# A hybrid attention and RG-LRU block on one core: the first stages written out in order for all five engines, with fewer, larger weight loads and two gates moved in between the compression products

## The chip, the cores and the metric

The kernel runs on one core of a Trainium2 chip. The metric is the device time of one execution in microseconds (us), as the median of several runs. Engines are named as in the profile: PE (TensorE), ACT (ScalarE), DVE (VectorE), POOL (GpSimd), SP (the engine that here only issues transfers).

## What is computed

One layer of a decoder: sequence 512, width 1024, float32. The input is normed; one wide projection gives queries, six key and value projections, gates and the recurrent branch. The stretch that the change touches is the norm, those projections, and `compress_blocks` (32 tokens of 64 channels, in steps of 16, through a small two-layer net), called once for keys and once for values:

```
def rms_norm(x, w):
    var = jnp.mean(xf * xf, axis=-1, keepdims=True)
    return (xf * lax.rsqrt(var + EPS) * w.astype(jnp.float32)).astype(x.dtype)
...
    xn = rms_norm(x, norm1_w[l])
    z = xn @ w_in[l]
    (q, k_c, v_c, k_s, v_s, k_w, v_w, g_nsa, xr, gr, g_a, g_b) = jnp.split(z, IN_SPLITS, axis=-1)
...
    blocks = jnp.concatenate([kb[:, :-1], kb[:, 1:]], axis=2) + pos[:, None, :]
    flat = blocks.transpose(0, 1, 3, 2, 4).reshape(B, nc, N_KV_GROUPS, CMP_BLOCK * HEAD_DIM)
    c = jax.nn.gelu(flat @ w1) @ w2
...
    merged = jax.nn.sigmoid(g_a) * (attn @ w_up_attn[l]) + jax.nn.sigmoid(g_b) * (rnn @ w_up_rnn[l])
    x = x + merged @ w_out[l]
    hn = rms_norm(x, norm2_w[l])
    x = x + jnp.square(jax.nn.relu(hn @ mlp_w1[l])) @ mlp_w2[l]
```

Behind the projections come attention over compressed, selected and windowed keys (8 heads, 4 blocks of 128 queries), the recurrence, the merge, and a squared-ReLU MLP.

## The kernel before, in words

**Precision.** Each float32 product is three matmuls: every operand is split into a rounded part (hi) and the rest (lo), and PE adds hi·hi, lo·hi and hi·lo. A unit such as `k0`, `kc` or a gate `g` is 8 blocks of 128 rows times 3 matmuls of 128x512: 24 matmuls (`unit_mm`, L422 to L424: weight hi, weight lo, activation lo).

**Weights.** A weight tile is 128x1024 (512 KB). From job 4 on it comes twice: POOL issues a load into `whi` (L191), ACT writes minus its rounded part into `wlo` (L218), and POOL issues a second load that adds the source to it (L219). Only the four query tiles come raw (`wraw`, SP's queue, L201) and are split by ACT (L361) and DVE (L363).

**Order of the first stages.** PE and SP follow the written order. ACT, DVE and POOL are ordered by a scheduler. The written order on PE is: warm-up (L115); 96 query matmuls (L381), with the sum of squares (`n_ss`, L325) and the broadcast of the norm's factor (`n_b`, L343) near their end; `k0`, `k1`; 96 matmuls of `v` (L520 to L522); and then what the string `MID = "kvSTcccccccc"` says: `kc`, `vc` (k, v), start of the attention lanes (S scores, T transposes and products), eight compression units (c, 8 matmuls `hid` each, L630). After it come 16 gates `g`. Lanes go one step ahead at each `tick()`; in `unit_mm` a tick comes after every `step[0]` blocks, and `GSTEP = (2,) * 16` gives 6 fill matmuls per tick in all gates.

**The norm.** ACT squares `xT` (L369), POOL adds the squares up (`sqa`, L366 and L370), PE sums over partitions (L325), POOL takes the power (L337). `q`, `k0`, `k1`, `v`, `kc`, `vc` are multiplied out from the un-normed input `xwh`/`xwl`, and the factor `rb` (L389) is applied when they leave the accumulator; the gates use the normed input `xnh`/`xnl` (L401 to L403; POOL makes `xnl`). DVE gathers `kc` and `vc` into the block layout `T` while multiplying by `rb` (L570, 16 instructions of 64x248), and ACT and DVE split `T` into `tc` (L574, L575). The finish of a compression unit (`hs` L580, `hq`, `hx`, `kp`) is a chain over ACT, DVE and PE.

Of the kernel before, what the change touches and what calls it, by code (L numbers as in the profile page):

```python
# [7 lines left out]
F32 = mybir.dt.float32  # L8
# [7 lines left out]
P = 128  # L16
# [29 lines left out]
KLP = "dp"  # L46
QLP = "dd"
# [4 lines left out]
MID = "kvSTcccccccc"  # L52
# [10 lines left out]
CLO = "ppdd" * 4  # L63
GSTEP = (2,) * 16
# [11 lines left out]
def kernel(ctx: ExitStack, tc: tile.TileContext, a, out: bass.AP):  # L76
# [9 lines left out]
    ctx.enter_context(tc.manual_schedule(engines={nc.tensor.engine, nc.sync.engine}))  # L86

# [38 lines left out]
    def job(src, n=1024, lo="dd", hi="aa"):  # L126
        jobs.append((src, n, lo + hi))
# [3 lines left out]
    job(a["wz"][0])  # L131
    job(a["wz"][1])
    VK = ((0, 3), (3, 6), (6, 8))
    for k0, k1 in VK:
        job(a["wv"][:, k0 * 280:k1 * 280], (k1 - k0) * 280)
    job(a["wz"][2])
    job(a["wz"][3])
    mid = {"g": [a["wz"][t] for t in range(20, 36)], "c": [a["cw1"][c] for c in range(8)]}
    for x in MID:
        if x in mid:  # L140
            job(mid[x].pop(0), lo=CLO[2 * (7 - len(mid["c"])):][:2] if x == "c" else "dd")
    for w in mid["g"]:
        job(w)
    tail = [a["wz"][4 + 2 * c + kind] for kind, c in RORDER] + [a["wua"][n] for n in range(4)]
    for n, w in enumerate(tail):
        if XA <= n < XB:
            job(w, lo=XLO, hi=XHI)
        else:
            job(w)
# [26 lines left out]

    def dma_to(i):
        while nxt["dma"] <= min(i, len(jobs) - 1):
            n = nxt["dma"]
            src, w, _ = jobs[n]  # L180
            if isinstance(src, tuple):
# [7 lines left out]
            if n >= 4:  # L189
                hi = wt("whi")  # L190
                pool.dma_start(hi[:, :w], src)  # L191
                raws[n] = hi
                nxt["dma"] += 1
                continue
            r = wt("wraw", F32)
            raws[n] = r
            if n < 4:
                for h in range(2):
                    k = 2 * n + h
                    sp.dma_start(xT[k], a["xT"][k])  # L200
                    sp.dma_start(r[:, h * S:(h + 1) * S], a["wq"][k])  # L201
# [9 lines left out]
    def conv_to(i, parts=1):  # L211
        while nxt["conv"] <= min(i, len(jobs) - 1):
# [3 lines left out]
            if not isinstance(src, tuple):  # L216
                hi, lo = raws[n], wt("wlo")
                act.activation(lo[:, :w], f(hi[:, :w]), AF.Copy, scale=-1.0)  # L218
                pool.dma_start(lo[:, :w], src, accum_op=OP.add)  # L219
                convs[n] = (hi, lo)  # L220
# [99 lines left out]
    def ss_mm(sqs, nt, name):  # L320
        ps = pt("av", name + "_ss", [P, nt])
        n = len(sqs)
        for m, sq in enumerate(sqs):
            for i in range(nt):
                pe.matmul(ps[:, i:i + 1], lhsT=sq[:, i * P:(i + 1) * P], rhs=ones[:, 0:1],  # L325
                          start=(m == 0 and i == 0), stop=(m == n - 1), skip_group_check=True)
        return ps

    def ss_pow(ps, nt, power, name, r=None):
# [4 lines left out]
        if power == -1:  # L334
            dve.reciprocal(r, ms)
        else:
            pool.tensor_tensor(r, ms, mhalf[:, :nt], op=OP.pow)  # L337
# [8 lines left out]

    sqa = tt("sqa")
    qps = [pt("mm", "q0"), pt("mm", "q1"), pt("s", "q2"), pt("s", "q3")]
    rb = const.tile([P, S], F32, name="rb")
    xwh, xwl, wq = [], [], []  # L350
    for k in range(KD):
        if k % 2 == 0:
            raw = raws[k // 2]
            wh2 = wt("whi")
            wl2 = wt("wlo")
            nxt["use"] += 1
            nxt["conv"] += 1
# [16 lines left out]
    rc = const.tile([P, NT], F32, name="rc")
    rch = const.tile([P, NT], F32, name="rch")
    for k in range(KD):
        for t in range(3):
            for j in range(4):
                cs = slice(j * P, (j + 1) * P)
                l_, r_ = ((wq[k][0], xwh[k]), (wq[k][1], xwh[k]), (wq[k][0], xwl[k]))[t]  # L380
                pe.matmul(qps[j], lhsT=l_[:, cs], rhs=r_, start=(k == 0 and t == 0),  # L381
                          stop=(k == KD - 1 and t == 2))
        if k == 5:
            ss = ss_mm([sqa], NT, "n1")
            rs_ = ss_pow(ss, NT, -0.5, "n1", rc)
            dve.tensor_scalar(rch, rc, 0.5, None, op0=OP.mult)
        if k == 6:
            rb_ps = ss_bcast(rs_, NT, "n1")
            act.copy(rb, rb_ps)  # L389
    dma_to(4 + 3)  # L390
    conv_to(5)

    xnh, xnl = [], []
    for k in range(KD):
        xnh.append(rt("X", f"xnh{k}", F32R))
        xnl.append(rt("X", f"xnl{k}", F32R))

    def xn_lane():
        for k in range(KD):
            x32 = tt("x32")  # L400
            dve.scalar_tensor_tensor(x32, xT[k], v("n1", k), rb, op0=OP.mult, op1=OP.mult)  # L401
            act.copy(xnh[k], x32)
            pool.tensor_tensor(xnl[k], x32, f(xnh[k]), op=OP.subtract)  # L403
            yield

    qs = [rt("A", f"qs{h}", F32R) for h in range(NH)]

    def q_evac(j):
        q32 = tt("q32")
        dve.tensor_tensor(q32, qps[j], rb, op=OP.mult)  # L410
        e, o = qs[2 * j], qs[2 * j + 1]
        act.copy(e[0:64], q32[0:64])
        act.copy(o[64:128], q32[64:128])
        (pool if QLP[0] == "p" else dve).tensor_tensor(e[64:128], q32[0:64], f(e[0:64]), op=OP.subtract)
# [797 lines left out]
```

## Time and profile before

| what | value |
|---|---|
| median of 3 runs | 838.39 us (837.63 to 839.85) |
| profiled execution | 839.27 us |
| its span, first to last instruction | 837.6 us |
| PE busy | 788.0 us, 94% |
| DVE busy | 596.9 us, 71% |
| ACT, POOL busy | 439.2 us, 358.6 us |

The profiled execution is 1.7 us longer than its span: the time around the instructions. Read the profile by stages: the page's 40 slices show in which of them PE is not full, the table of stretches gives each stage's own busy times and granted clock, the waits of PE say what it waited for, and the timeline when each thing began.

### The profile page before, as it was taken

The numbers are of one execution on the slowest core, as the hardware profiler recorded it, in microseconds if no ns is written. First come the engines' busy times: TensorE is split into PE (matmuls) and PEld (weight loads), VectorE is DVE, ScalarE is ACT, GpSimd is POOL, SyncE is SP. The second block draws the span as 40 slices with busy tenths as digits, with TensorE's granted clock in tenths as the row PEclk, the third lists the DMA queues.
The fourth block names the chain that finished last, engine by engine and source line by source line (L and its number), as shares of the span: only waits on it lengthen the run. The fifth ranks groups of instructions, "written<-read, shape, count | busy, mean of one in ns | idle before, by whom it ended". The sixth has DMA issues, their size and how long they took to land. (4 is left out here: it accounts for less than half of the span.)

```text
span 837.6 us, 10414 instructions
## 1 busy us (share of the span) xinstructions
PE 788.0 (94%) x3626; PEld 640.5 (76%) x3626; DVE 596.9 (71%) x989; ACT 439.2 (52%) x793; POOL 358.6 (43%) x379
## 2 busy tenths in 40 slices
PE   6996599999999999999996999999999999999986
PEld 3895478877777888788884888788878888888764
DVE  8488435767776576776479847877777777777895
ACT  7255445655555689796343464444444444435343
POOL 5566322111111222222458228574747373736842
PEclk9998689999999999999997999999999999999988
DMA  6758996555444678778990574657575747486302
GB/s 212 186 138 190 249 234 146 106 115 106 102 101 105 154 159 191 173 163 173 206 300 11 182 171 76 165 131 178 126 188 118 194 108 204 97 232 146 102 0 100
DMA packets 43828, 126.43 MB, mean 151 GB/s; under 512 B 5120, under 2 KB 5376, under 8 KB 43776
## 3 DMA queue, kind: packets, MB, share of 16 engines
q0 software_dynamic: 26208, 94.58, 51.4%
q1 hardware_dynamic: 17568, 31.19, 11.3%
q8 instruction: 28, 0.46, 0.2%
q14 instruction: 24, 0.20, 0.1%
HBM read 123.66 MB, written 2.10 MB: 150 GB/s over the span
## 5 line engine op out<-in xcount | busy, mean ns | idle before, releaser
L218 ACT ACTIVATE wlo<-whi 128x1024 fp32r<-128x1024 f32 (+2 forms) x91 | 95.6, 1051 | 61.9 <-PE ur L423 12.2
L209 DVE TENSOR_TENSOR wlo<-braw,whi 128x512 fp32r<-128x512 f32 x120 | 97.1, 840 | 40.2 <-issue 35.2
L278 POOL TENSOR_TENSOR braw<-braw,braw 128x512 f32<-128x512 f32 x64 | 98.5, 1552 | 25.6 <-DVE wlo L209 22.7
L423 PE MATMUL h<-hnh,wlo 128*128 128x512 f32 x256 | 100.5, 392 | 2.1 <-DMA wlo<-in_w_dram 1.8
L422 PE MATMUL h<-hnh,whi 128*128 128x512 f32 x256 | 99.8, 390 | 0.0
L424 PE MATMUL h<-hnl,whi 128*128 128x512 f32 x256 | 99.7, 390 | 0.0
L206 ACT CAST whi<-braw 128x512 fp32r<-128x512 f32 x120 | 69.2, 615 | 57.2 <-POOL braw L278 41.2
L191 POOL DMA_DIRECT2D whi<-in_wz_dram x36 | 22.2, 616 | 162.2 <-PE g L424 118.0
L1079 DVE SCALAR_TENSOR_TENSOR x<-p,r,x 128x512 f32<-128x512 f32 x112 | 80.1, 741 | 3.1 <-PE p L1045 3.0
L423 PEld LDWEIGHTS h<-hnh,wlo 128*128 128x128 f32 x256 | 48.0, 188 | 14.7 <-DMA wlo<-in_w_dram 4.9
L424 PEld LDWEIGHTS h<-hnl,whi 128*128 128x128 f32 x256 | 48.1, 188 | 10.1 <-DVE hnl L1017 0.2
L422 PEld LDWEIGHTS h<-hnh,whi 128*128 128x128 f32 x256 | 48.1, 188 | 9.9
L422 PE MATMUL g<-xnh,whi 128*128 128x512 f32 x128 | 55.6, 434 | 0.0
L1045 PE MATMUL p<-whi,sl 128*128 128x512 f32 x128 | 50.7, 396 | 3.1 <-DVE sl L209 3.1
L1042 PE MATMUL p<-whi,sh 128*128 128x512 f32 x128 | 50.6, 396 | 2.0 <-ACT sh L206 2.0
L423 PE MATMUL g<-xnh,wlo 128*128 128x512 f32 x128 | 50.6, 395 | 1.3 <-DMA wlo<-in_wz_dram 1.3
L424 PE MATMUL g<-xnl,whi 128*128 128x512 f32 x128 | 50.9, 398 | 0.0
L1044 PE MATMUL p<-wlo,sh 128*128 128x512 f32 x128 | 50.4, 394 | 0.0
L721 DVE TENSOR_REDUCE mx<-sb 128x1 f32<-128x384 f32 (+3 forms) x44 | 28.2, 641 | 28.0 <-PE sb L718 27.8
L219 POOL DMA_DIRECT2D wlo<-in_w_dram x32 | 28.0, 876 | 43.6 <-ACT wlo L218 39.7
L1066 DVE TENSOR_TENSOR h<-h 128x512 f32<-128x512 f32 x32 | 38.3, 1198 | 11.2 <-ACT h L1065 11.2
L219 POOL DMA_DIRECT2D wlo<-in_wz_dram x36 | 31.9, 887 | 32.0 <-ACT wlo L218 29.0
(323 smaller groups left out, 2126.0 us busy)
## 6 DMA issues: line engine op xcount, KB each, us to landing
whi<-in_wz_dram POOLq DMA_DIRECT2D x36, 512.0 KB, 3.8
wlo<-in_wz_dram POOLq DMA_DIRECT2D x36, 512.0 KB, 7.0
braw<-in_w_dram SPq DMA_DIRECT2D x64, 256.0 KB, 5.2
whi<-in_w_dram POOLq DMA_DIRECT2D x32, 512.0 KB, 4.6
wlo<-in_w_dram POOLq DMA_DIRECT2D x32, 512.0 KB, 6.4
whi<-in_cw_dram POOLq DMA_DIRECT2D x8, 512.0 KB, 4.8
wlo<-in_cw_dram POOLq DMA_DIRECT2D x8, 512.0 KB, 8.1
whi<-in_wur_dram POOLq DMA_DIRECT2D x8, 512.0 KB, 3.6
```

Source lines behind the costliest of these rows:

```text
L206: act.copy(hi, src)
L209: (pool if eng == "p" else dve).tensor_tensor(lo, src, f(hi), op=OP.subtract)
L218: act.activation(lo[:, :w], f(hi[:, :w]), AF.Copy, scale=-1.0)
L219: pool.dma_start(lo[:, :w], src, accum_op=OP.add)
L278: pool.tensor_tensor(o, i0, i1, op=OP.subtract)
L422: pe.matmul(ps, lhsT=wh[:, c], rhs=ah[k][:, sl], start=(first and i == 0), stop=False)
L423: pe.matmul(ps, lhsT=wl[:, c], rhs=ah[k][:, sl], start=False, stop=False)
L424: pe.matmul(ps, lhsT=wh[:, c], rhs=al[k][:, sl], start=False, stop=(last and i == n - 1))
L1042: pe.matmul(ps, lhsT=ah[:, qs_], rhs=wh[:, ws], start=(fresh and m == 0), stop=False, skip_group_check=True)
L1044: pe.matmul(ps, lhsT=ah[:, qs_], rhs=wl[:, ws], start=False, stop=False, skip_group_check=True)
L1045: pe.matmul(ps, lhsT=al[:, qs_], rhs=wh[:, ws], start=False, stop=(end and m == 1), skip_group_check=True)
L1079: dve.scalar_tensor_tensor(x2[i][c], ps, 0.5 if n == "w" else r2[:, i:i + 1], x2[i][c], op0=OP.mult, op1=OP.add)
```

## The change

All five engines follow a written order from the start to the letter T in `MID`; after it ACT, DVE and POOL are ordered by the scheduler as before. Within that stretch:

- **Query preparation** goes block by block (k): ACT casts the weight, then the input; DVE takes both rests. The squares are taken by ACT from a second, row-wise copy of the input (`xq`, 8 loads of 256 KB on SP's queue), each with its row sum (`accum_out`); POOL's additions and the 8 `n_ss` matmuls go.
- **Weights.** Jobs 4 to 8 (`k0`, `k1`, `v`) and the eight compression tiles (`cw1`) come once, raw, on SP's queue, and are split by ACT (cast) and DVE (subtract). `v`'s and the compression's raw tiles share two buffers ("big"). `kc`, `vc` and the gates keep the two loads on POOL's queue.
- **POOL's arithmetic** on `sqa`, `xnl` and `kl` goes; DVE makes `xnl` and `kl`, ACT copies the mirrored half of `kl`.
- **`kc` and `vc`** are multiplied from the normed input, so the gather into `T` needs no factor; ACT does it, as 16 copies.
- **`MID`** puts gate `g0` ahead of the compression units and `g1` between its halves, and starts the lanes there. The last three gates tick after every block: 3 fill matmuls per tick.

```diff
-MID = "kvSTcccccccc"
+MID = "kvgccccSTgcccc"
+EAHEAD = (0, 0)
...
-GSTEP = (2,) * 16
+GSTEP = (2,) * 13 + (1,) * 3
...
+    early = tc.manual_schedule(engines={pe.engine, sp.engine, act.engine, dve.engine, pool.engine})
+    early.__enter__()
...
+    job(a["wz"][0], by="hw")
+    job(a["wz"][1], by="hw")
+        job(a["wv"][:, k0 * 280:k1 * 280], (k1 - k0) * 280, by="hw")
...
+    def load(n):
+        src, w, _ = jobs[n]
+        if n in hw:
+            raws[n] = const.tile([P, 1024], F32, name="vraw", tag="big", bufs=2) if n > 5 else wt("wraw", F32)
+            sp.dma_start(raws[n][:, :w], src)
+        else:
+            raws[n] = wt("whi")
+            pool.dma_start(raws[n][:, :w], src)
...
+    def conv(n):
+        src, w, _ = jobs[n]
+        if n in hw:
+            hi, lo = wt("whi"), wt("wlo")
+            q = w // 2
+            for m in range(2):
+                sl = slice(m * q, (m + 1) * q)
+                act.copy(hi[:, sl], raws[n][:, sl])
+                pump(1, lambda sl=sl: dve.tensor_tensor(
+                    lo[:, sl], raws[n][:, sl], f(hi[:, sl]), op=OP.subtract))
+            pump(0)
+        else:
+            hi, lo = raws[n], wt("wlo")
+            act.activation(lo[:, :w], f(hi[:, :w]), AF.Copy, scale=-1.0)
+            pool.dma_start(lo[:, :w], src, accum_op=OP.add)
+        convs[n] = (hi, lo)
...
+    xq = {}
+    for i in range(NT):
+        for c in range(2):
+            xq[i, c] = tt(f"xq{i}{c}")
+            sp.dma_start(xq[i, c], a["xt"][i, c])
+    posr = const.tile([P, 2, 16], F32, name="posr")
+    sp.dma_start(posr, a["pos"])
+    craw = []
+
+    def c_load():
+        t = const.tile([P, 1024], F32, name=f"craw{len(craw)}", tag="big", bufs=2)
+        sp.dma_start(t, a["cw1"][len(craw)])
+        craw.append(t)
...
+    def ss_pow(ps, nt, name, r):
         ms = st(name + "_ms", [P, nt])
-        dve.tensor_scalar(ms, ps, 1.0 / D, EPS, op0=OP.mult, op1=OP.add)
-        if r is None:
-            r = st(name + "_r", [P, nt])
...
-        if k == 0:
-            pool.tensor_tensor(sqa, xT[k], xT[k], op=OP.mult)
-        else:
-            sq = tt("sq")
-            act.activation(sq, xT[k], AF.Square)
-            pool.tensor_tensor(sqa, sqa, sq, op=OP.add)
...
-            pool.tensor_tensor(xnl[k], x32, f(xnh[k]), op=OP.subtract)
...
+        next(consts, None)
+    for i in range(NT):
+        for c in range(2):
+            act.activation(xq[i, c], xq[i, c], AF.Square, accum_out=ssq1[:, i, c:c + 1])
...
+            conv(4)
+            rs_ = ss_pow(ssq1, NT, "n1", rc)
+            dve.tensor_scalar(rch, rc, 0.5, None, op0=OP.mult)
+        if k == 5:
+            conv(5)
+        if k == 6:
+            rb_ps = ss_bcast(rs_, NT, "n1")
+            act.copy(rb, rb_ps)
+            conv(6)
+            conv(7)
+            load(9)
+            load(8)
+            c_load()
+        if k == 1:
+            load(4)
+            load(5)
+            load(6)
+            load(7)
...
+    def xn_part(k0, k1):
+        for k in range(k0, k1):
+            x32 = tt("x32")
+            dve.scalar_tensor_tensor(x32, xT[k], v("n1", k), rb, op0=OP.mult, op1=OP.mult)
+            act.copy(xnh[k], x32)
+            pump(1, lambda k=k, x32=x32: dve.tensor_tensor(xnl[k], x32, f(xnh[k]), op=OP.subtract))
...
+    conv(9)
+    load(10)
+    xn_part(0, 4)
     xw_unit("k0", lambda ps: k_evac(ps, 0), "t")
+    xn_part(4, 6)
+    conv(8)
+    c_load()
+    load(11)
+    conv(10)
+    xn_part(6, 8)
     xw_unit("k1", lambda ps: k_evac(ps, 1), "t")
-    lanes.append(xn_lane())
+    pump(0)
+    conv(11)
...
-                for m in range(2):
-                    o_ = T[w][hf * 64:hf * 64 + 64, m * 8:m * 8 + 8, g, 0:NCB - 1].rearrange("p j n -> p n j")
-                    dve.tensor_tensor(o_, pv[:, m:m + NCB - 1, hf::2], rv[:, m:m + NCB - 1, hf::2], op=OP.mult)
-        for c in range(4):
-            t = ring.tile([P, 4, 2, DH], F32R, name=f"tc{c}", tag="T", bufs=8)
-            src = T[w][:, c * 4:c * 4 + 4].rearrange("p j g n -> p j (g n)")
-            act.copy(t[:, :, 0], src)
-            dve.tensor_tensor(t[:, :, 1], src, f(t[:, :, 0]), op=OP.subtract)
...
+        for m in range(2):
+            if m and not w:
+                conv(12)
+            T = tt("T", [P, 8, NG, NCB])
+            for g in range(NG):
+                dve.tensor_copy(T[:, :, g, NCB - 1], posr[:, w, m * 8:m * 8 + 8])
+            for g in range(NG):
+                pv = ps[g * 64:g * 64 + 64].rearrange("p (n s) -> p n s", s=16)
+                for hf in range(2):
+                    o_ = T[hf * 64:hf * 64 + 64, :, g, 0:NCB - 1].rearrange("p j n -> p n j")
+                    act.copy(o_, pv[:, m:m + NCB - 1, hf::2])
+            for c in (2 * m, 2 * m + 1):
+                t = ring.tile([P, 4, 2, DH], F32R, name=f"tc{c}", tag="T", bufs=8)
+                src = T[:, (c % 2) * 4:(c % 2) * 4 + 4].rearrange("p j g n -> p j (g n)")
+                act.copy(t[:, :, 0], src)
+                pump(1, lambda t=t, src=src: dve.tensor_tensor(t[:, :, 1], src, f(t[:, :, 0]), op=OP.subtract))
+                tc_[w, c] = t
...
+    def c_split():
+        n = c_split.n
+        if n == 8:
+            return
+        c_split.n += 1
+        hi, lo = wt("chi"), wt("clo")
+        for m in range(2):
+            sl = slice(m * S, (m + 1) * S)
+            act.copy(hi[:, sl], craw[n][:, sl])
+            pump(1, lambda sl=sl: dve.tensor_tensor(lo[:, sl], craw[n][:, sl], f(hi[:, sl]), op=OP.subtract))
+        cconv.append((hi, lo))
+        if len(craw) < 8:
+            c_load()
+    c_split.n = 0
...
+    extra = {"k": lambda: (load(12), c_split()), "v": c_split, "g": c_split}
     for x in MID + "g" * (16 - MID.count("g")):
+        if ng < 1 and x in extra:
+            extra[x]()
         if x == "c":
+            if not cconv:
+                c_split()
+            pump(0)
             next(cmp)
+            c_split()
+            if len(craw) > 5 and 13 not in raws:
+                load(13)
+            if len(craw) > 6 and 13 not in done:
+                conv(13)
             tick()
         elif x == "T":
+            pump(0)
+            early.__exit__(None, None, None)
+            ahead[:] = DMA_AHEAD, CONV_AHEAD
             lanes.append(tr_lane())
         elif x == "S":
             lanes.append(s_lane())
         elif x == "k":
-            xw_unit("kc", lambda ps: t_evac(ps, 0), "av")
+            z_unit("kc", lambda ps: t_evac(ps, 0), "av")
         elif x == "v":
-            xw_unit("vc", lambda ps: t_evac(ps, 1), "av")
+            z_unit("vc", lambda ps: t_evac(ps, 1), "av")
```

**ACT in the query preparation.** In these rows `whi` is the cast of a query weight block, `xwh` that of an input block, `sq` a square. Before:

```order
L362 ACTIVATE xwh_135<-xT_93,vec 128x512
L362 ACTIVATE xwh_142<-xT_94,vec 128x512
L362 ACTIVATE xwh_153<-xT_95,vec 128x512
L369 ACTIVATE sq<-xT_94 128x512
L369 ACTIVATE sq<-xT_95 128x512
L362 ACTIVATE xwh_162<-xT_96,vec 128x512
L369 ACTIVATE sq<-xT_96 128x512
L362 ACTIVATE xwh_173<-xT_97,vec 128x512
L369 ACTIVATE sq<-xT_97 128x512
L361 CAST whi<-wraw 128x512 x6
```

Now:

```order
L437 CAST whi<-wraw 128x512
L438 ACTIVATE xwh_170<-xT_96,vec 128x512
L401 ACTIVATE ez<-ez 128x8
L437 CAST whi<-wraw 128x512
L438 ACTIVATE xwh_185<-xT_99,vec 128x512
L437 CAST whi<-wraw 128x512
```

The first weight cast stood behind five input casts and four squares; now it is the first of the stage, and no square stands ahead of a cast.

**ACT at the end of the compression's first half.** `hs` is the copy that begins the finish of the key half, `pr` an exponential of the score lane, `chi` the cast of a raw compression tile. Before:

```order
L218 ACTIVATE wlo<-whi 128x1024
L727 ACTIVATE pr,sm<-sb,nb 128x128 x8
L218 ACTIVATE wlo<-whi 128x1024
L580 COPY hs<-hid_811 128x256
L218 ACTIVATE wlo<-whi 128x1024
L206 CAST th<-tp 128x512
```

Now:

```order
L854 CAST chi<-craw_792 128x512 x2
L854 CAST chi<-craw_851 128x512 x2
L193 ACTIVATE wlo<-whi 128x1024
L854 CAST chi<-craw_895 128x512 x2
L854 CAST chi<-craw_913 128x512 x2
L626 COPY hs<-hid_881 128x256
L773 ACTIVATE pr,sm<-sb,nb 128x128 x8
```

`hs` and the first exponentials now stand behind the casts of the sixth and seventh raw tile (895 and 913).

**PE in one slot of the last three gates.** `g` are the fill matmuls, `av` a product of the attention lane, `sb` a score product, `tp` transposes. Before:

```order
L422 MATMUL g_2456<-xnh_342,whi 128x512
L423 MATMUL g_2456<-xnh_342,wlo 128x512
L424 MATMUL g_2456<-xnl_343,whi 128x512
L422 MATMUL g_2456<-xnh_344,whi 128x512
L423 MATMUL g_2456<-xnh_344,wlo 128x512
L424 MATMUL g_2456<-xnl_345,whi 128x512
L762 MATMUL av<-th,vs_489 128x512
L762 MATMUL av<-tl,vs_489 128x512
L714 MATMUL sb<-kh_427,qs_361 128x512
L716 MATMUL sb<-kl_428,qs_361 128x512
L718 LDWEIGHTS identb
L718 MATMUL sb<-tri,identb 128x128
```

Now:

```order
L508 MATMUL g_2430<-xnh_415,whi 128x512
L509 MATMUL g_2430<-xnh_415,wlo 128x512
L510 MATMUL g_2430<-xnl_416,whi 128x512
L808 MATMUL av<-th,vs_584 128x512
L808 MATMUL av<-tl,vs_584 128x512
L760 MATMUL sb<-kh_503,qs_428 128x512
L762 MATMUL sb<-kl_504,qs_428 128x512
L764 LDWEIGHTS identb
L764 MATMUL sb<-tri,identb 128x128
L793 MATMUL tp<-ident,pr 128x128 x4
```

Three of the six fill matmuls in a slot are gone; the lane's own matmuls are the same.

## Rows read from the trace of the kernel before

**Rows 1.** The page: busy time by engine, and the granted clock in 40 slices.

```profile
PE 788.0 (94%) x3626; PEld 640.5 (76%) x3626; DVE 596.9 (71%) x989; ACT 439.2 (52%) x793; POOL 358.6 (43%) x379
...
PEclk9998689999999999999997999999999999999988
```

**Rows 2.** Stretches in us; length, busy PE, PEld, DVE, ACT, POOL; clock, DMA share, GB/s.

```profile
0.00:12.32 12.32, 4.45 (x10) 1.34 (x10) 9.18 (x29) 8.01 (x16) 5.12 (x10) 1.00 0.84 288
12.32:38.59 26.27, 26.10 (x111) 21.17 (x112) 15.11 (x16) 10.31 (x17) 16.34 (x20) 1.00 0.65 176
38.59:49.70 11.11, 11.11 (x51) 9.20 (x49) 9.03 (x12) 8.17 (x14) 5.68 (x6) 1.00 0.64 150
49.70:62.05 12.35, 12.35 (x98) 12.35 (x96) 12.18 (x12) 7.21 (x11) 9.44 (x9) 1.00 0.47 97
62.05:75.84 13.79, 7.15 (x26) 5.54 (x25) 11.67 (x16) 6.23 (x15) 9.74 (x10) 0.75 0.82 185
75.84:81.79 5.95, 5.74 (x25) 4.43 (x24) 5.65 (x12) 2.39 (x6) 2.77 (x3) 1.00 0.99 208
81.79:111.07 29.28, 19.94 (x116) 18.01 (x114) 13.44 (x42) 15.21 (x39) 10.44 (x15) 0.71 1.05 245
111.07:120.00 8.93, 7.66 (x28) 5.97 (x28) 3.01 (x15) 3.50 (x13) 2.41 (x4) 0.81 1.03 244
213.50:271.30 57.80, 57.80 (x300) 44.75 (x298) 40.17 (x100) 32.11 (x69) 8.42 (x12) 1.00 0.51 108
```

**Rows 3.** Waits of PE from 0 to 130 us: total, times, longest.

```profile
PE hid L630 <- DMA wlo<-in_cw_dram: 9.3, 6, 4.3
PE kc L423 <- DMA wlo<-in_wz_dram: 6.6, 1, 6.6
PE q L381 <- ACT whi L361: 6.6, 1, 6.6
PE g L423 <- DMA wlo<-in_wz_dram: 1.3, 1, 1.3
```

**Rows 4.** Timeline around the first query matmul: start, duration, what.

```profile
4.11 0.72 ACT L362 ACTIVATE xwh<-xT,vec 128x512 fp32r<-128x512 f32 x1 [1.03 <-DMA xT<-in_xT_dram]
...
12.33 2.08 PE L381 MATMUL q<-xwh,whi 128*128 128x512 f32 x4 [6.63 <-ACT whi L361]
...
17.86 1.09 PE L381 MATMUL q<-xwh,whi 128*128 128x512 f32 x4
```

**Rows 5.** The query's raw weight tiles: from issue to landing.

```profile
DMA to landing us min/median/max: 3.0/5.2/5.6
```

**Rows 6.** Groups of ACT, 0 to 130 us: busy us, mean ns.

```profile
L412 ACT CAST qs<-q 64x512 fp32r<-64x512 f32 x4 | 2.5, 622 | 0.2
...
L580 ACT COPY hs<-hid 128x256 f32<-128x256 f32 x2 | 0.7, 374 | 1.6 <-PE hid L630 1.6
```

**Rows 7.** Groups of DVE, 0 to 130 us, in the same columns.

```profile
L401 DVE SCALAR_TENSOR_TENSOR x<-xT,vec,rb 128x512 f32<-128x512 f32 x8 | 11.8, 1526 | 0.0
...
L570 DVE TENSOR_TENSOR T<-kc,rb 64x248 f32<-64x248 f32 x8 | 4.2, 603 | 2.4 <-PE kc L424 2.3
...
L575 DVE TENSOR_TENSOR tc<-T,tc 128x256 fp32r<-128x256 f32 x8 | 2.9, 420 | 0.1
...
L410 DVE TENSOR_TENSOR q<-q,rb 128x512 f32<-128x512 f32 x4 | 2.6, 684 | 4.4 <-PE q L381 4.4
```

**Rows 8.** Transfers from 0 to 130 us: size, median us from issue to landing.

```profile
wlo<-in_cw_dram POOLq DMA_DIRECT2D x8, 512.0 KB, 8.1
```

**Rows 9.** Timeline of PE in `kc`: spacing of matmuls at the low and at the full clock.

```profile
70.10 0.63 PE L422 MATMUL kc<-xwh,whi 128*128 128x512 f32 x1
70.53 0.63 PE L423 MATMUL kc<-xwh,wlo 128*128 128x512 f32 x1
...
72.66 0.39 PE L423 MATMUL kc<-xwh,wlo 128*128 128x512 f32 x1
72.89 0.40 PE L424 MATMUL kc<-xwl,whi 128*128 128x512 f32 x1
```

More of the change, by code (lines that the diff above doesn't have):

```diff
@@ L175 @@
     nxt = {"dma": 0, "conv": 0, "use": 0}
+    def load(n):
[22 more added lines that the diff above has]
+        convs[n] = (hi, lo)
+        done.add(n)
+    done = set()
     def dma_to(i):
@@ L180, in dma_to @@
             src, w, _ = jobs[n]
+            if n >= 4 and not isinstance(src, tuple):
+                if n not in raws:
+                    load(n)
+                nxt["dma"] += 1
+                continue
             if isinstance(src, tuple):
@@ L216, in conv_to @@
             if not isinstance(src, tuple):
[L217 to L220, printed above, removed]
+                if n not in done:
+                    conv(n)
             else:
@@ L318 @@
     dve.memset(mhalf, -0.5)
[L320 to L329, printed above, removed]
-        ms = st(name + "_ms", [P, nt])
-        dve.tensor_scalar(ms, ps, 1.0 / D, EPS, op0=OP.mult, op1=OP.add)
-        if r is None:
-            r = st(name + "_r", [P, nt])
[L334 to L337, printed above, removed]
+    def ss_pow(ps, nt, name, r):
+        ms = st(name + "_ms", [P, nt])
+        dve.tensor_tensor(ms, ps[:, :, 0], ps[:, :, 1], op=OP.add)
+        dve.tensor_scalar(ms, ms, 1.0 / D, EPS, op0=OP.mult, op1=OP.add)
+        pool.tensor_tensor(r, ms, mhalf[:, :nt], op=OP.pow)
         return r
@@ L374 @@
[L374 to L389, printed above, removed]
@@ new lines, with q_evac, lo, unit_mm @@
+    qs = [rt("A", f"qs{h}", F32R) for h in range(NH)]
+    def q_evac(j):
+        q32 = tt("q32")
+        dve.tensor_tensor(q32, qps[j], rb, op=OP.mult)
+        e, o = qs[2 * j], qs[2 * j + 1]
+        act.copy(e[0:64], q32[0:64])
+        act.copy(o[64:128], q32[64:128])
+        def lo():
+            dve.tensor_tensor(e[64:128], q32[0:64], f(e[0:64]), op=OP.subtract)
+            dve.tensor_tensor(o[0:64], q32[64:128], f(o[64:128]), op=OP.subtract)
+        pump(1, lo)
+    def unit_mm(ps, w, ah, al, ks, first=True, last=True, sl=slice(0, S), o=0, ticks=True):
+        wh, wl = w
+        n = len(ks)
+        for i, k in enumerate(ks):
+            c = slice(o + i * P, o + (i + 1) * P)
+            pe.matmul(ps, lhsT=wh[:, c], rhs=ah[k][:, sl], start=(first and i == 0), stop=False)
+            pe.matmul(ps, lhsT=wl[:, c], rhs=ah[k][:, sl], start=False, stop=False)
+            pe.matmul(ps, lhsT=wh[:, c], rhs=al[k][:, sl], start=False, stop=(last and i == n - 1))
+            if ticks and i % step[0] == step[0] - 1 and i < n - 1:
+                tick()
@@ L482, with full_unit, z_unit, xw_unit @@
+    def full_unit(ah, al, name, evac, tag="mm"):
+        w = wnext()
+        ps = pt(tag, name)
+        unit_mm(ps, w, ah, al, range(KD))
+        evac(ps)
+        tick()
+    def z_unit(name, evac, tag="mm"):
+        full_unit(xnh, xnl, name, evac, tag)
+    def xw_unit(name, evac, tag):
+        full_unit(xwh, xwl, name, evac, tag)
     kh, kl = {}, {}
@@ L817 @@
         tick()
+    ahead[:] = DMA_AHEAD, CONV_AHEAD
     step[0] = XSTEP
```

193 lines of the change are left out of this document (72 added, 121 removed).

## The prediction

> **What bounds the kernel now.** Read the page's first lines before anything else [rows 1]: PE is busy 788.0 us of 837.6, so nearly all of the time is matmuls that this change keeps, and at most some 50 us can be won. The slices of the granted clock show where PE is not full: the digits below 9 stand almost all in the first seventh. The table of stretches [rows 2] puts numbers on it. [...] `k0`/`k1` and `v` (38.59 to 62.05) have no gap. The waits of PE [rows 3] name the causes: a cast of the query weights by ACT (6.6 us), then second loads of weight tiles, `kc` (6.6), `hid` (9.3 in six waits) and `g` (1.3). [...] So the change attacks what ends last there. The question is what is late next.
>
> **Part 1, the start of the queries.** PE starts them at 12.33, behind the cast at 11.67; ACT had taken all input casts and squares first [rows 4]. The first raw tile is there at about 4.7 (issued at 1.7, fastest landing 3.0 us [rows 5]). With the new order come a weight cast (0.62, as 512 columns of `qs` take [rows 6]) and an input cast (0.72 [rows 4]), hence PE from about 6.2. That is 6.1 us earlier. Later blocks arrive about one a microsecond and PE takes 12 x 0.23 = 2.8 us each (17.86, four matmuls in 0.92), so they keep ahead. The twelve slow matmuls at the start (12.33 to 17.86, 5.5 us for what takes 2.8 later) I leave as they are. They and 84 at 0.23 make 24.8 of the stretch's 26.27 [rows 2]; the other 1.5 are `n_ss` and `n_b`, and with the 8 `n_ss` matmuls 0.9 of it goes. The new cost is the norm's chain: eight row-wise loads of 256 KB come behind the 4 MB of query tiles and inputs. At the first stretch's 288 GB/s the 6 MB end near 22 us, the raw `k0` tile near 23.5; a cast of 1.2, a subtraction of 0.69, sum and power (1.4) give the factor at about 27.7, and PE asks for it after seven blocks, at 6.2 + 2.7 + 7 x 2.8 = 28.5 at the latest. Eight squares on ACT at 0.6 lie beside PE. **Gain 7.0**; 5 if the factor comes 2 us late, 8.5 if the slow start shrinks too. The queries then end near 31.5.
>
> **Part 2, `k0`, `k1`, `v`.** Same matmuls, 23.5 us [rows 2], no gap before. What covers them: raw tiles loaded long ahead, and DVE, which now has POOL's subtractions too. I count 36 instructions of 0.684 [rows 7] between the queries' end and the last `xnl` (12 for `qs`, 6 for the keys, 16 for the normed input, 2 for the last `v` tile), 24.6 us: done at about 56, and `kc` needs its last block at 60. DVE's 1526 ns for 128x512 [rows 7] were taken beside POOL's work, which goes; at that price the eight products of the normed input alone would end 6.7 us later, which is in the third rival below. **Gain 0**; `v` ends at about 55.0.
>
> **Part 3, `kc` and `vc`.** They lasted 62.05 to 81.79, 19.7 us, for 48 matmuls that `k0` and `k1` do in 11.1 [rows 2]. Their tiles still come twice, but the queue ahead of them is shorter by five tiles and eight, and I place the second loads at 52 to 60, at or before their need. **Gain 8.6**; 5 if a second load is 3.6 us late.
>
> **Part 4, compression and two gates.** Equal work before: 29.28, plus 11.1 for two gates, plus what the first gate lost, 8.93 - 28 x 0.231 = 2.4 [rows 2], so 42.8. The pure work at the full clock is 19.94 x 0.71 = 14.2 plus 11.1, so 25.3. But each raw tile passes a chain: load 5.2, two casts 1.24, a subtraction 0.69, 7.1 us, two buffers, so one tile per 3.6 us against 0.95 us of matmuls. Three tiles are ready when `g0` begins; the other five need 18 us, and `g1` covers 5.5 of that. ACT adds to it: the 16 gather copies (the nearest row is 128x256 copied from the accumulator, 0.374 [rows 6]; the strided gather on DVE took 0.603 where a plain 128x256 took 0.420 [rows 7], so up to 0.54), eight tile splits, and the finish `hs` and the first exponentials, which stand behind the sixth and seventh tile's casts. Walking that order with these durations, PE waits four times for 2 to 3 us, 9.5 in all, and I add 2.6 for matmuls at the low clock after them (spacing 0.43 for 0.23 [rows 9]). New time 25.3 + 9.5 + 2.6 = 37.4. **Gain 5.4**; 17.5 with no wait left, a loss of 3 if loads take 8.1 us as the second loads do.
>
> [...] I keep 0.374 since nothing shows ACT doing such a copy.
>
> **Part 5, the late gates.** Two gates have gone from the attention's cover, so 24 slots keep 3 fill matmuls where they had 6. They took 57.80 us, PE full [rows 2], 2.41 each. Without 72 x 0.226 = 16.3 us of fill, PE has 41.5 us left; DVE is busy 40.2 us in the same stretch and loses nothing. Both need nearly the whole of a slot, 1.73 and 1.67, and hand over to each other within it, so they won't pack. I take a slot of about 1.92: PE waits 0.19 in each. **Loss 4.5**; nothing at best, 16.3 if a slot stays at 2.41.
>
> Behind it nothing changes: later weight tiles are loaded as before. The sum is 7.0 + 8.6 + 5.4 - 4.5 = 16.5, so 839.27 - 16.5 = 822.8 for an execution like the profiled one. That one stands 0.9 above the median of 838.39, so I forecast **822**.
>
> **Rivals.**
> - *The compression's waits vanish.* The raw loads may land faster now that nothing comes twice (DMA share 1.05 before), and ACT's copies may be cheap. Then 12.1 us more: 810. Against it stands the order on ACT, casts ahead of `hs`, which no faster load removes. Chance 0.20.
> - *The late gates stay latency-bound.* If score, maximum, exponential, transposes and product form a chain of 2.4 us per slot, the fill was free before: 11.8 us worse, 834. For it: no slot of the profile is shorter than 2.41 us, so how long the lane's own chain is does not show. Against it: the lane works several blocks ahead. Chance 0.12.
> - *The change doesn't do what it says:* PE is still released late at its weights, since 2 MB of extra input stands ahead of the raw tiles on SP's queue and DVE holds the chain of subtractions. With the factor 3 us late, and `kc` 4.5 us late for the normed input: 7.5 worse, 829. Chance 0.10.
> - *Slower: the late gates at the low clock.* [...] Chance 0.04. [...]
> - The last 0.04: gains and losses cancel to no change.
>
> **How the numbers follow.** The forecast has 0.50. A measurement of this kernel can tell about 0.3%, 2.5 us, from no change, that is 836 to 841. Forecast and the first three rivals lie below it; of the late-gates case, which spreads over some 831 to 838, 0.02 falls within. Faster: 0.50 + 0.20 + 0.10 + 0.10 = 0.90. Same: 0.02 + half of the last case, 0.04. Slower: the low clock and the other half, 0.06. The range reaches to the vanishing waits below (810, and 2 for the slow start) and to the late gates above: **808 to 834**. What it leaves out is the low clock, the cancelled case and some of the edges of the two end cases, under 0.2.
>
> **What would show it.** Right: the first query matmul at 6 to 7 us; no wait of PE for `kc`; no `hid` wait on a second load, but some on `chi` or ACT; `vc` ending at 64 to 68; PE in the late gates below 98% with DVE above 85%, clock 1.00. Wrong in part 1 or 3: a wait of PE at `n_b` or at the first `xnl` of over 2 us. Wrong in part 4: the two gates and eight units lasting over 43 us. Wrong in part 5: slots of 2.4 us, or a granted clock under 0.9 there.

## The result and the profile after

The changed kernel takes 813.11 us (median of 4 runs, 811.42 to 815.10) against 838.45 us before: a ratio of 0.9697, with a 95% interval of 0.9670 to 0.9724. That is 25 us less. The forecast was 822, in a range of 808 to 834.

The page's first lines, the counterpart of [rows 1]: PE is busy 7.6 us less though its work is the same but for 8 small matmuls, so it ran less at the low clock (the execution's mean granted clock is 0.986 for 0.971); POOL lost 49 us.

```profile
PE 780.4 (96%) x3618; PEld 633.6 (78%) x3618; DVE 585.6 (72%) x1016; ACT 452.7 (56%) x835; POOL 309.2 (38%) x329
...
PEclk9999999999999999999998999999999999999989
```

The stretches of the changed kernel, in the columns of [rows 2]. In order: up to the first query matmul, the queries, `k0`/`k1`, `v`, `kc` and `vc`, then the eight compression units with two gates (63.39 to 97.92), the rest up to the product of the attention's output (97.92 to 345.43), and, as a part of that, the late gates' 24 slots.

```profile
0.00:6.15 6.15, 3.92 (x11) 1.29 (x11) 1.08 (x6) 3.13 (x6) 1.49 (x9) 1.00 0.62 197
6.15:29.11 22.96, 22.96 (x105) 18.94 (x105) 16.94 (x47) 18.18 (x40) 1.16 (x2) 1.00 0.83 308
29.11:39.99 10.88, 10.88 (x50) 9.01 (x48) 10.51 (x17) 6.84 (x11) 2.11 (x3) 1.00 0.46 130
39.99:52.49 12.50, 12.50 (x97) 12.38 (x96) 11.43 (x20) 9.26 (x17) 1.43 (x2) 1.00 0.56 160
52.49:63.39 10.90, 10.90 (x51) 9.01 (x49) 6.05 (x21) 10.66 (x23) 1.44 (x2) 1.00 0.80 171
...
63.39:97.92 34.53, 27.47 (x164) 23.85 (x162) 19.94 (x59) 27.45 (x68) 6.41 (x10) 0.95 0.70 201
97.92:345.43 247.51, 245.74 (x1220) 195.39 (x1218) 172.90 (x401) 166.42 (x317) 42.60 (x60) 1.00 0.63 135
...
197.69:244.08 46.39, 44.87 (x243) 33.13 (x242) 38.97 (x101) 28.26 (x65) 3.99 (x6) 1.00 0.37 80
```

The same work ends at 371.22 us in the kernel before and at 345.43 here, 25.8 us earlier; behind it both run alike (466.4 and 466.8 us). So the whole gain lies ahead of that point, the first matmul of the attention's output product:

| part | before | after | gain | forecast |
|---|---|---|---|---|
| queries end | 38.59 | 29.11 | 9.5 | 7.0 |
| `k0`, `k1`, `v` | 23.46 | 23.38 | 0.1 | 0 |
| `kc`, `vc` | 19.74 | 10.90 | 8.8 | 8.6 |
| from there to 371.22 / 345.43 | 289.43 | 282.04 | 7.4 | 0.9 (5.4 - 4.5) |

The waits of PE from 52 to 104 us, where `kc`, `hid` and `g` waited for second loads before [rows 3]: no DMA is left, and what is late next is ACT's cast of a raw compression tile.

```profile
PE hid L676 <- ACT chi L854: 5.8, 2, 5.1
PE tp L793 <- DVE pr L784: 0.7, 1, 0.7
PE hid L676 <- DVE clo L855: 0.6, 2, 0.3
```

### The profile page after: what moved, and what is told of

Read it like the earlier page. It is cut to its first block, busy times and chain, and to the rows that moved or that the text cites. A ratio compares the mean times of both kernels' runs of the same rounds, so it can differ in the third digit from the quotient of the medians.

```text
span 812.2 us, 10431 instructions
## 1 busy us (share of the span) xinstructions
PE 780.4 (96%) x3618; PEld 633.6 (78%) x3618; DVE 585.6 (72%) x1016; ACT 452.7 (56%) x835; POOL 309.2 (38%) x329
## 5 line engine op out<-in xcount | busy, mean ns | idle before, releaser
L193 ACT ACTIVATE wlo<-whi 128x1024 fp32r<-128x1024 f32 x78 | 82.5, 1059 | 44.7 <-PE ur L509 12.3
L178 POOL DMA_DIRECT2D whi<-in_wz_dram x34 | 19.9, 587 | 171.5 <-PE g L510 120.3
L194 POOL DMA_DIRECT2D wlo<-in_wz_dram x34 | 30.1, 886 | 65.4 <-ACT wlo L193 60.5
L773 ACT ACTIVATE pr<-sb,nb 128x128 f32<-128x128 f32 (+3 forms) x64 | 33.5, 527 | 17.8 <-DVE nb L768 17.0
```

## The experiments

Each takes the changed kernel (unless it says otherwise) and alters a few lines of it. Medians are compared by their ratio to the kernel before, run beside it on the same chip; the change itself has 0.9697 (0.9670 to 0.9724). No run gives POOL its arithmetic back or takes the row-wise squares out by themselves, so the share of these two parts of the change is not shown.

### One load or two

**`twice`**: five weight tiles loaded twice again.

```diff
-    job(a["wz"][0], by="hw")
-    job(a["wz"][1], by="hw")
+    job(a["wz"][0])
+    job(a["wz"][1])
...
-        job(a["wv"][:, k0 * 280:k1 * 280], (k1 - k0) * 280, by="hw")
+        job(a["wv"][:, k0 * 280:k1 * 280], (k1 - k0) * 280)
```

> Edit: the five weight tiles of k0, k1 and v come twice again on POOL's queue (load, minus the rounded part by ACT, second load that adds), in the same written order; the compression tiles stay raw. My theory: PE waits 1 to 3 us at the second loads of k0 and k1, and v's second loads take DMA time from kc's: 814 to 818. Rival: everything is loaded far enough ahead, and one load or two makes no difference here: 812 to 814.

Measured: 823.02 us, ratio 0.9809 (0.9773 to 0.9845): some 9 us of the gain go, more than expected, and in part at another place. The waits of PE and the row-wise input's transfers in this run:

```profile
PE n_b L375 <- POOL rc L369: 4.6, 1, 4.6
PE v L575 <- DMA wlo<-in_wv_dram: 3.7, 1, 3.7
```

```profile
L347 SPq DMA_DIRECT2D xq<-in_xt_dram x8: 327/328/328, 10.3 to 15.0; - x8
...
DMA to landing us min/median/max: 5.4/8.0/11.2
```

In the change these transfers all land in 5.4 us. Here the doubled weight loads run beside them, the last lands after 11.2, ACT's squares wait 5.2 us for them, and PE waits 4.6 us for the norm's factor. Then `v` waits 3.7 us for a second load. After each of these waits some matmuls run slower: the first four of the queries behind `n_b` take 1.71 us where the next four take 1.09, and `v`'s follow each other at 0.23 us from 60.50 to 63.53 where they did at 0.13 before the wait (the granted clock is 0.86 from 52.00 to 64.00). So `vc` ends 11.6 us later than in the change; some of it comes back behind. The expected waits at `k0` and `k1` did not come.

**`ctwice`** and **`cpool`**: the compression tiles, twice from POOL's queue, and once from POOL's queue.

```diff
     def c_load():
-        t = const.tile([P, 1024], F32, name=f"craw{len(craw)}", tag="big", bufs=2)
-        sp.dma_start(t, a["cw1"][len(craw)])
+        t = wt("chi")
+        pool.dma_start(t, a["cw1"][len(craw)])
...
     def c_split():
...
-        hi, lo = wt("chi"), wt("clo")
-        for m in range(2):
-            sl = slice(m * S, (m + 1) * S)
-            act.copy(hi[:, sl], craw[n][:, sl])
-            pump(1, lambda sl=sl: dve.tensor_tensor(lo[:, sl], craw[n][:, sl], f(hi[:, sl]), op=OP.subtract))
+        hi, lo = craw[n], wt("clo")
+        act.activation(lo, f(hi), AF.Copy, scale=-1.0)
+        pool.dma_start(lo, a["cw1"][n], accum_op=OP.add)
```

```diff
-        sp.dma_start(t, a["cw1"][len(craw)])
+        pool.dma_start(t, a["cw1"][len(craw)])
```

> Edit: the eight compression tiles come twice again on POOL's queue instead of once raw on SP's; ACT writes minus the rounded part, DVE's subtraction goes; order otherwise as in the change. My theory: PE waits for second loads again, some 5 to 6 us each with four to six of them not covered, as in the kernel before: 818 to 826. Rival: ACT's queue is the limit in the compression either way, and the time stays within 2 us of 813.1.

> Edit: the eight raw compression tiles are loaded once, as in the change, but issued by POOL instead of SP; ACT and DVE split them as in the change. My theory: what cost 24 us when they came twice is the second load and its place behind ACT's instruction; one load from POOL's queue costs a few us, where its issue stands behind a second load of a gate's tile: 813 to 818. Rival: POOL's queue itself, in order and shared with the gates' loads, is the cost: 822 or more.

Measured: `ctwice` 836.99 us, ratio 0.9980 (0.9963 to 0.9997), nearly all of the gain lost; `cpool` 813.95 us, 0.9722 (0.9708 to 0.9737), 2 us or nothing. So for these tiles the queue matters little or not at all; the second load does. `ctwice` is slower than I expected. Its waits, 63 to 122 us, and POOL's timeline show why:

```profile
PE hid L676 <- DMA clo<-in_cw_dram: 20.9, 5, 5.7
```

```profile
77.81 0.86 POOL L853 DMA_DIRECT2D clo<-in_cw_dram  x1 [5.71 <-ACT clo L852]
78.36 0.89 POOL L354 DMA_DIRECT2D chi<-in_cw_dram  x1
...
87.01 0.90 POOL L853 DMA_DIRECT2D clo<-in_cw_dram  x1 [5.64 <-ACT clo L852]
87.56 0.90 POOL L354 DMA_DIRECT2D chi<-in_cw_dram  x1
```

A tile's second load waits for ACT, and the next tile's first load is written behind it on the same queue: load, ACT, load become one chain. This order was written for one load, so the 24 us are the price of two loads in this order, not in the best one.

### The written order

**`sched`**: ACT, DVE and POOL left to the scheduler.

```diff
-    early = tc.manual_schedule(engines={pe.engine, sp.engine, act.engine, dve.engine, pool.engine})
-    early.__enter__()
...
-            early.__exit__(None, None, None)
```

> Edit: ACT, DVE and POOL are ordered by the scheduler from the start, as in the kernel before; everything else of the change stays. My theory: the edits carry the gain (one load in place of two, squares off the critical order, gates as cover) and the order of writing is close to what a scheduler does: within 4 us of 813.1. Rival: the written order itself carries it, above all at the start: the scheduler puts input casts ahead of the first weight cast, the queries start at 9 us or later instead of 6.2, and PE waits more in the compression: 820 or more.

Measured: 820.14 us, ratio 0.9769 (0.9746 to 0.9792), 6 to 7 us slower. The rival was right on the place, at the start, and on the price, but not in the compression. The timeline shows input casts ahead of the first weight cast again, as in [rows 4]:

```profile
10.44 0.72 ACT L436 ACTIVATE xwh<-xT,vec 128x512 fp32r<-128x512 f32 x1 [0.64 <-DMA xT<-in_xT_dram]
11.07 3.20 ACT L435 CAST whi<-wraw 128x512 fp32r<-128x512 f32 x6
11.72 2.07 PE L453 MATMUL q<-xwh,whi 128*128 128x512 f32 x4 [6.03 <-ACT whi L435]
```

Some of the loss comes back: `vc` ends 8.0 us later than in the change, but the wait for a cast that costs PE 5.1 us there costs 2.8 us here. So the worth of the written order lies at the start; behind it the scheduler did no worse.

### Gates in the compression, and the late gates

**`nogate`** takes the two gates out of the compression; **`bmid`** puts two gates into it in the kernel before; **`gstep2`** undoes the finer ticks.

```diff
-MID = "kvgccccSTgcccc"
+MID = "kvccccSTcccc"
```

```diff
-MID = "kvSTcccccccc"
+MID = "kvgccccSTgcccc"
```

```diff
-GSTEP = (2,) * 13 + (1,) * 3
+GSTEP = (2,) * 16
```

> Edit: the two gates are taken out of the compression again and stand behind it with the others (order kc, vc, four units, lanes start, four units, gates). My theory: g0 and g1 cover the time in which ACT gathers and casts; without them PE waits for casts 5.5 us more before the first unit and about 3 to 5 us more between the halves; a part comes back in the late gates: 819 to 824. Rival: the gates only moved, and what they covered is covered by the lanes' work: within 2 us of 813.1.

> Edit, in the kernel before: only the order string, so that one gate stands ahead of the compression units and one between the halves; loads, squares and engines as before. My theory: two gates as cover are worth little while every tile comes twice, because each gate brings two loads of 512 KB of its own into a stretch whose DMA engines are full already: within 4 us of 838.4. Rival: they cover the waits as they do in the change, where taking them out cost 9.7 us: 828 to 832.

> Edit: the last three gates tick every two blocks again (6 fill matmuls per lane slot instead of 3). My theory: 12 lane steps fewer are taken by the gates; the lanes must reach the end of their score part before the recurrent units may start, so these steps run bare, with about 1 us of PE waiting each: slower by 6 to 12 us than 813.1, about 822. Rival: the steps go along with the recurrent units, which tick too, and the time stays within 1.5 us of 813.1, or falls by the 1.5 us that PE waits in the late gates now.

Measured: `nogate` 822.79 us, ratio 0.9799 (0.9772 to 0.9825). The time is as expected, the reason only in part. PE's waits for the casts grow from 5.8 to 10.6 us, by 4.8, where I had expected 8.5 to 10.5; beside them the granted clock falls to 0.71 over the whole part:

```profile
PE hid L676 <- ACT chi L854: 10.6, 4, 4.7
PE hid L676 <- DVE clo L855: 0.3, 1, 0.3
```

```profile
64.15:105.00 40.85, 29.44 (x144) 25.88 (x143) 20.76 (x61) 27.20 (x68) 5.36 (x9) 0.71 0.59 163
```

`bmid` 847.36 us, ratio 1.0115 (1.0096 to 1.0135): the same string makes the kernel before **slower** by 10 us; I had expected no change, the rival a gain. Its stretches, one from `g0` to the end of the eight units and one from there on:

```profile
83.62:126.61 42.99, 30.00 (x155) 25.95 (x155) 13.50 (x43) 17.59 (x45) 12.90 (x18) 0.80 0.93 207
126.61:379.10 252.49, 247.84 (x1227) 196.84 (x1225) 172.88 (x401) 167.69 (x318) 44.05 (x62) 1.00 0.63 136
```

With tiles coming twice the two gates hide nothing (42.99 us; the same units and two gates behind them took an estimated 42.8 before). The loss lies behind: 252.49 us there, where the kernel before took an estimated 246.6. Of PE's 252.49 - 247.84 = 4.7 us of waits, 1.1 (for a gate's second load) and 1.4 (for `gr`) stand in the kernel before too. What is new is a stretch between the last gate and the recurrent units:

```profile
258.49:273.55 15.06, 13.11 (x67) 8.03 (x66) 11.87 (x30) 10.54 (x25) 1.41 (x2) 1.00 0.33 71
```

With two gates fewer to tick in, lane steps are left over and run bare, that is without fill. Another 1.7 us of the profiled execution's loss was there before the string could matter on PE: `vc` ends at 83.5 for 81.8. `gstep2` has such a bare stretch by itself: 816.90 us, ratio 0.9735 (0.9702 to 0.9768), 3 to 4 us slower. Its lanes run bare for 14.43 us, in which PE waits 1.9:

```profile
229.37:243.80 14.43, 12.49 (x64) 7.50 (x64) 11.87 (x30) 9.90 (x25) 1.25 (x2) 1.00 0.35 73
```

The price per bare step is smaller than I thought. So the gates as cover paid only with tiles that come once, and they want the finer ticks in the gates that are left. The kernel before with both the string and the finer ticks was not tried.

### What bounds the compression now

**`tsplit`**, **`tsplit2`** (half of the gather's copies on DVE, by source group, then by target partitions) and **`xw`** (`kc`, `vc` from the un-normed input, all 16 on DVE with the factor):

```diff
-                    act.copy(o_, pv[:, m:m + NCB - 1, hf::2])
+                    if g == 0:
+                        act.copy(o_, pv[:, m:m + NCB - 1, hf::2])
+                    else:
+                        dve.tensor_copy(o_, pv[:, m:m + NCB - 1, hf::2])
```

```diff
-                    act.copy(o_, pv[:, m:m + NCB - 1, hf::2])
+                    (act.copy if hf == 0 else dve.tensor_copy)(o_, pv[:, m:m + NCB - 1, hf::2])
```

```diff
-                    act.copy(o_, pv[:, m:m + NCB - 1, hf::2])
+                    dve.tensor_tensor(o_, pv[:, m:m + NCB - 1, hf::2], rv[:, m:m + NCB - 1, hf::2], op=OP.mult)
...
-            z_unit("kc", lambda ps: t_evac(ps, 0), "av")
+            xw_unit("kc", lambda ps: t_evac(ps, 0), "av")
```

> Edit: of the 16 copies that gather kc and vc into the block layout, 8 go from ACT to DVE. My theory: the one long wait of PE that is left in the compression (5.1 us at 76.0, for the cast of the third raw tile) is ACT's queue, which is full from 59 to 78 because each copy takes 0.60 us; 8 copies less free 4.8 us ahead of that cast, the wait shrinks to 1 us or less, and the time falls by 4 to 5 us from 813.1, to about 808.5. Rival: the raw tiles' loads and DVE's rests end last there; then the cast comes no earlier in effect and the time stays within 1.5 us of 813.1.

> Edit: of the 16 gather copies the 8 that write the upper 64 partitions of T go to DVE, the 8 of the lower partitions stay on ACT. (In the run before, with the split by source group, DVE's copies began only when ACT's of the same tile had ended, and ACT waited for DVE afterwards: nothing ran side by side.) My theory: now ACT's queue is 4.8 us shorter ahead of the cast of the third raw tile, PE's wait of 5.1 us there falls to 1 us or less, and the later loads start sooner too: 808 to 810. Rival: the landing of the raw tiles, or the chain copies, cast, rest, ends last all the same: 812 to 814.

> Edit: kc and vc are multiplied from the un-normed input again, and DVE gathers into T with the factor (16 two-input instructions of 0.60 us) in place of ACT's 16 copies. My theory: the normed input buys nothing on PE, since kc did not wait for anything before either but its weights; ACT's queue gets 9.6 us shorter, DVE has the time: 808 to 811, as with the split copies. Rival: DVE's gather becomes the chain that ends last (it took 0.60 us each before, too): 813 to 817.

Measured: 813.92, 812.72 and 812.48 us; ratios 0.9701, 0.9688 and 0.9694, all within the change's interval. My theory failed three times, and the rivals, that the rests or the gather end last all the same, were nearer. The timeline of `tsplit2` shows the first reason:

```profile
69.90 0.60 ACT L616 COPY T<-vc 64x248 f32<-64x248 f32 x1
70.53 0.60 DVE L616 COPY T<-vc 64x248 f32<-64x248 f32 x1 [0.29 <-ACT T L616]
71.16 0.57 ACT L616 COPY T<-vc 64x248 f32<-64x248 f32 x1 [0.66 <-DVE T L616]
```

The two engines take turns, each waiting for the other's copy, so sharing the gather out saves little. Their copies read the same accumulator and write the same tile `T`; which of the two makes the wait is not shown. PE's wait for the cast does get shorter, but its waits for DVE's rests, 0.6 us in the change, take over most of that:

```profile
PE hid L676 <- ACT chi L854: 4.2, 2, 3.1
PE hid L676 <- DVE clo L855: 2.0, 2, 1.7
```

`xw` shows the second reason: whichever engine gathers, ACT's next instructions (`tc`, then the cast of the third raw tile) stand behind the gather of `vc`. Its waits come out alike, 3.9 us for casts and 1.9 for rests. The result is also that the normed input and the engine of the gather, changed together, are worth nothing measurable here.

**`ord`** and **`ord2`** move casts ahead of that gather, and `ord2` also two casts behind the finish:

```diff
+            if w:
+                c_split()
...
-    extra = {"k": lambda: (load(12), c_split()), "v": c_split, "g": c_split}
+    extra = {"k": lambda: (load(12), c_split()), "v": c_split}
```

```diff
-            c_split()
+            if c_split.n < 6 or ng > 1:
+                c_split()
```

> Edit: on ACT (and DVE) the splits of the third and fourth raw compression tiles are written ahead of, and between, the two halves of the gather of vc; nothing else. The two runs with the gather shared out showed ACT's and DVE's copies from the same accumulator one after the other, so sharing gains nothing, and vc's gather itself is not needed until the fifth unit. My theory: it is the written order on ACT that holds the third unit, and with the casts first PE's wait of 5.1 us becomes 1 to 2 us: 808 to 810. Rival: the raw tile is not there earlier, or the wait moves to the fifth unit, which needs vc's gather: within 1.5 us of 813.1.

> Edit: as the run ord, and two further casts (seventh and eighth raw tile) are written behind the start of the key half's finish instead of ahead of it, so that the finish and the first exponentials do not wait for those tiles' landing. My theory: with them out of the way PE's waits at the exponentials and at the sixth to eighth unit shrink by another 1 to 2 us: 807 to 809. Rival: the last units then wait for the later casts instead and lose what the exponentials gain: equal to ord or up to 2 us above it.

Measured: `ord` 817.51 us, ratio 0.9772 (0.9748 to 0.9795), slower than the change; `ord2` 811.91 us, 0.9699 (0.9684 to 0.9713), equal to it. The wait aimed at did shrink, from 5.1 to 2.5 us, but ACT's tanh of `g0` now stands behind the gather, and in `ord` the finish behind a later cast. The waits of `ord`:

```profile
PE hid L678 <- ACT chi L856: 2.5, 1, 2.5
PE hq L633 <- ACT hs L628: 2.0, 1, 2.0
PE g L508 <- ACT tg L843: 1.7, 1, 1.7
```

`ord2` takes the second one away. Two of its stretches: the gate `g1`, and the whole that has the same units as 63.39 to 97.92 in the change:

```profile
79.30:90.14 10.84, 10.84 (x44) 9.24 (x45) 5.55 (x16) 6.24 (x22) 1.98 (x3) 0.71 0.74 207
...
64.23:98.74 34.51, 29.75 (x164) 25.75 (x162) 18.23 (x53) 27.11 (x68) 6.07 (x10) 0.85 0.77 219
```

PE waits 34.51 - 29.75 = 4.8 us, against 34.53 - 27.47 = 7.1 in the change, and takes the same time: for the same 164 matmuls it is busy 2.3 us longer, at a granted clock of 0.85 against 0.95. After its two waits (2.3 us up to 75.0, 1.7 up to 79.3) `g1` has 0.71; in the change, after one wait of 5.1 up to 76.0, the units behind it run at 0.56 up to 79.90, and `g1` has 1.00. This is one execution, and the slowest of `ord2`'s five: 814.38 us at a mean granted clock of 0.981, where the other four took 811.03 to 812.74 us at 0.984 to 0.986. So it shows that a low clock can give back what shorter waits won; that this is why the medians are equal is not shown. No version was found that beats the change.

## Why the prediction was right, point by point

**Right: what ended last, and that it goes.** The change removes the waits it was said to remove. `kc` and `vc` came out at 8.8 for 8.6, `k0` to `v` at 0.1 for 0, the first query matmul at 6.15 for 6.2. Of the signs that I gave for being right, two were missed by a little: `vc` ended at 63.39, not at 64 to 68, since part 1 gained more, and DVE was busy 84% in the late gates, not above 85%. The whole came out 9 us below the forecast because parts 1, 4 and 5 all erred the same way. It came near the 810 of the first rival, but not for its reason: the waits in the compression did not vanish.

**Part 1 was too small, 9.5 for 7.0**, and above the 8.5 that I gave as its end. The start and `n_ss` were right; the term I left as it was failed, "the twelve slow matmuls at the start". They took 5.5 us before and take 2.85 here (6.15 to 9.00):

```profile
6.15 1.20 PE L455 MATMUL q<-xwh,whi 128*128 128x512 f32 x4 [0.98 <-ACT xwh L438]
...
9.00 1.07 PE L455 MATMUL q<-xwh,whi 128*128 128x512 f32 x4
```

That is 2.7 us, so 8.5 was too low even for the case that it named: 7.0 + 2.7 = 9.7. In `sched`, where PE again waits 6.0 us ahead of them, the first four take 2.07 us again, as the 2.08 of the kernel before after a wait of 6.6 [rows 4]; in the change, after a wait of 1.0, they take 1.20. So in these three executions the slow start goes with the late start. The rows don't say how: the granted clock reads 1.00 over the first twelve in all three, although in `sched` they take 5.28 us, 0.44 each, about the spacing of the low clock in [rows 9], 0.43. The norm's factor, too, was better than I thought, and cost no more than 0.3 us. It was there at 25.3, just when PE asked, not at 27.7 (the terms I gave for that add up to 26.8): the row-wise loads had landed by 20.4, not near 22.

**Part 4 was too small, 8.3 for 5.4** (42.8 - 34.53). The waits had the cause I named, in fewer pieces: 7.1 us of them in all, for 9.5, and PE was busy 27.47 us, 2.2 more than the 25.3 of pure work, where I had added 2.6 for the low clock. The raw tiles landed in a median of 3.9 us, where I counted 5.2 [rows 5], or 8.1 at worst [rows 8]:

```profile
craw<-in_cw_dram SPq DMA_DIRECT2D x8, 512.0 KB, 3.9
```

The price of ACT's gather copies was wrong the other way, 0.604 and 0.582 us where I took 0.374:

```profile
L616 ACT COPY T<-kc 64x248 f32<-64x248 f32 x8 | 4.8, 604 | 0.1
L616 ACT COPY T<-vc 64x248 f32<-64x248 f32 x8 | 4.7, 582 | 0.1
...
L626 ACT COPY hs<-hid 128x256 f32<-128x256 f32 x2 | 0.7, 372 | 0.0
```

Here the higher price, up to 0.54, which I had estimated from DVE's gather and its plain instruction [rows 7] and not used, was the better guide: on ACT too the strided 64x248 takes 0.58 to 0.60 us against 0.372 for the plain 128x256. The copy steps through the accumulator that it reads as well as through the tile that it writes, and no run shows which of the two, if either, makes the price. ACT was busy 13.95 of 16.51 us from 63.39 to 79.90. That this gather is what PE's one long wait hangs on follows from `ord`, where the wait halves once the casts stand ahead of it; that cheaper copies would help was not tried.

**Part 5 came out at 1.5 for 4.5**, and the slot at 46.39 / 24 = 1.93 us for 1.92, the second by accident. I divided a stretch of 138 fill matmuls, 23 slots, by 24, which left PE 41.5 us of work for 24 slots; it has 44.87. Nor was 2.41 the shortest slot of the kernel before: the one from 263.40 to 265.69 takes 2.29. And PE waits only 1.5 us in the 24 slots: DVE at 38.97 of 46.39 and PE pack better than I thought. The clock stayed at 1.00. From the end of units and gates to the table's last points (371.22 and 345.43) the change takes 247.5 us where the kernel before took about 246.6, a loss of 0.9; a wait of 1.4 us for `gr`, which the kernel before has behind its gates, is gone. The 8.3 of part 4 and this loss make the 7.4 of the table.

**The rivals.** That the compression's waits vanish: no, 7.1 us are left. That the late gates stay at 2.41 us per slot: no. That raw loads come late behind the extra input: not in the change; `twice` shows the reverse, the extra input late behind doubled weight loads, with 4.6 us of waiting for the factor. That the late gates fall to the low clock, the case with 0.04: no. No run shows that term; the granted clock there is 1.00 in the change, through 1.5 us of scattered waits in 46.39, and it is 1.00 as well in the bare stretches of `gstep2` and `bmid`, where PE waits 1.94 and 1.95 us (14.43 - 12.49, 15.06 - 13.11). In the compression a low clock does come after waits, 0.71 in `ord2`'s `g1` after 2.3 and 1.7 us, and there, in the profiled execution, it ate what `ord2` had won.

## What to carry to other kernels

A tile that is loaded twice to be split costs a transfer, a place in a queue behind another engine, and the next tile's load behind that; one raw load and two engine instructions were worth more here than the written order (9 us for five weight tiles and 24 for the compression's, in an order written for one load, against 6 to 7), and for the compression's tiles the issuing queue made 2 us or nothing. Cover and supply have to be changed together: the gates as fill won 10 us once tiles came once, and nothing in the stretch itself while they came twice. Count PE's busy time beside its waits before believing a shorter wait: an engine in its written order hands the wait on, and a low clock can give it back (2.3 us in the profiled execution of `ord2`, at 0.85 for 0.95).

## What I had not expected of the hardware

- ACT and DVE took the same time for the strided 64x248 gather, 0.58 to 0.60 us, although DVE also multiplied in the kernel before [rows 7].
- DVE's subtraction of 128x512 took 1.30 us on average while POOL worked beside it, and 0.688 once POOL's arithmetic was gone; the product of the normed input went from 1.526 [rows 7] to 0.746. The trace of the kernel before has both prices: the subtractions at 18.41 and 19.02, beside no arithmetic of POOL, took 0.68 us, the one at 12.74, beside POOL's, 1.77. At 1.526 the eight products alone would have taken 6.2 us more of DVE's time beside `k0` to `v`. The first line is of the kernel before, the others of the change:

```profile
L363 DVE TENSOR_TENSOR wlo<-wraw,whi 128x512 fp32r<-128x512 f32 x8 | 10.0, 1301 | 0.0
...
L485 DVE SCALAR_TENSOR_TENSOR x<-xT,vec,rb 128x512 f32<-128x512 f32 x8 | 5.9, 746 | 0.1
L439 DVE TENSOR_TENSOR wlo<-wraw,whi 128x512 fp32r<-128x512 f32 x8 | 5.5, 688 | 4.9 <-ACT whi L437 4.9
```

- Less waiting did not mean less time: in the profiled execution of `ord2`, 2.3 us of waits removed came back as 2.3 us of slower matmuls.
